# A decoder block on one Trainium2 core: the down products of its feed-forward stage with tokens on the output partitions, and its last group finished tile by tile

## The chip, the core and the metric

The kernel runs on one core of a Trainium2 chip. Its time is the device time of one execution in microseconds (us). A profile records when each instruction of the five engines ran: TensorE (PE for its matmuls, PEld for its weight loads), VectorE (DVE), ScalarE (ACT), GpSimd (POOL) and SyncE (SP, which only issues DMAs here). The span is the time from the first to the last recorded instruction. The matmul computes out = stationary.T @ moving: the stationary operand is 128x128 and is loaded into the array, the moving operand (128 x 256 or 128 x 512 in this kernel) streams through it, and the partitions of the output are the columns of the stationary operand.

## What is computed

One decoder block on x of 512 tokens x 2048 columns, in float32. The part that matters here is its end; what stands before (normalisation, one input projection, two kinds of attention, output projection) is left out.

```python
S, D_MODEL, FFN_HIDDEN = 512, 2048, 5632
...
hn2 = rmsnorm(h, norm2_g[l])
h = h + (jax.nn.silu(hn2 @ w_gate[l]) * (hn2 @ w_up[l])) @ w_down[l]
return rmsnorm(h, final_g)        # x * rsqrt(mean(x*x) + 1e-6) * g, over the 2048 columns
```

## The kernel before

**Precision.** Each float32 operand of a matmul is split into a high and a low part (float32r), and a product is three matmuls: high x high, high x low, low x high (`mm3` at L297 to L299, `mm` at L302 to L304). The high part of a weight tile is written by ACT (L176, `Job.first`), the low part by DVE (L190, `Job.second`); a Twin does the same for two half-size pieces (L210 on ACT, L214 on DVE). The products of blocks are grouped in Strassen's way: seven products of sums of blocks (P1 to P7) instead of eight.

**Order.** All work is laid out by hand. `jobs` lists the weight tiles in the order in which TensorE uses them; `next_half` hands out the next split tile and first makes ACT and DVE split a few tiles ahead. `later(n, f)` issues f when n more tiles have been handed out, `soon` and `tick` do so by the number of products. DMAs of weights are issued on SP in the order of `units`, into five buffers `raw`; DMAs that add to memory go through POOL.

**The feed-forward stage.** The hidden 5632 columns are 44 slices f of 128 (FB = 44), in groups of PH = 4. For each f the seven quad products (gate and up, 24 matmuls of 128x256 each) run, and the results become activations of 128 hidden columns x 512 tokens. When a group of four slices is done, its down products follow, mixed into the next slices: for the first ten groups, `down7` does seven products for each of 8 column blocks k, 2 x 3 matmuls each. There the weights are stationary (128 hidden x 128 output columns) and the activations move (128 hidden x 256 tokens), so the output has 128 output columns on the partitions and 256 tokens along a row. ACT copies between the banks and out to staging tiles (L1690), POOL adds these to `kept_sums` in memory (L1697).

**Places in SBUF.** Tiles start at a multiple of 256 bytes, and operands stand at a chosen offset in them, in float32 elements: activations (moving) at MH = ML = 32, which is 128 bytes, weights (stationary) at WH = WL = 16, which is 64 bytes, or with `even` at 128 bytes too:

```python
MH, ML, WH, WL = 32, 32, 16, 16
...
    def wsplit(even):
        return both(wp, 512, MH if even else WH, tag=turn("w", 5), name="w")
```

The first product P1 of the slices f = 0, 2, all odd f and all f divisible by four has its first weight tile `even`; of the down products of a group, two of the 29 Twins are `even` too (one with a single product of 6 matmuls, one with two, 12 matmuls).

**The residual and the end.** The residual h is in memory during the stage. Scaled by DVE (L1863), it is added to `kept_sums` at f = 5, 6, 9, 10, 13, 14, 17 and 18 (`add_residual`). The scale per token stands along the row there, so it is spread over the partitions by matmuls with the identity (`Spread`, L379). At f = 41 and 42 `bring_back` loads the sums into `hs`. The last group, p = 10, is done in `last` without Strassen's grouping: for each half of the tokens (256) and each of 16 column blocks, 4 x 3 matmuls of 128x256 into `pl`, a DVE addition (L1985 or L1987), a square on ACT (L1962), a sum of squares on POOL or DVE (L1964) and a multiplication by the gain on ACT (L1965). The sum over the partitions and its inverse root (`Rsqrt`, matmuls at L350) and its spreading (`Spread`, L379) go through TensorE, for the first half of the tokens amid the second half's products, for the second half after the last product; then nine scalings on DVE (L1952) with their output DMAs (L1953) end the kernel.

## Time and profile before

| | |
|---|---|
| time, median of 3 runs | 2085.97 us (2085.27 to 5372.69) |
| the profiled execution | 2088.05 us, of which the span is 2086.3 us |
| mean granted TensorE clock | 0.998 |
| busy: PE / PEld / DVE / ACT / POOL | 99% / 96% / 84% / 65% / 19% |
| matmuls | 16297 |
| feed-forward stage, from its first quad product to the last down matmul | about 797 to 2073.6 us |
| after the last down matmul | 12.7 us |

A row of a list by line has the line, engine, operation, out<-in with shapes, the count, the busy time and the mean time of one in ns, and the idle time before. A row of the table by stretch has the stretch, its length, then for each engine the busy time and (x the number of instructions), the granted clock, the share of DMA time and GB/s. A row of the timeline has the start, the duration, the engine and the instruction. Matmuls are pipelined: one lasts longer than the time between two starts, so their pace is read from the starts.

### The profile page before, as it was taken

The page shows a single profiled execution, that of the slowest core. Times are in us where ns is not written, and L with a number is a line of the kernel's source. Part 1 is how long each engine was busy: PE and PEld are TensorE (multiplying, and loading weights), DVE is VectorE, ACT ScalarE, POOL GpSimd, SP SyncE. Part 2 cuts the span into 40 slices and gives each one's busy share as a digit, 9 for nine tenths or more (in the row PEclk, how much of TensorE's full clock was granted, in tenths as well). Part 3 has the DMA queues.
Part 4 walks back from the last instruction along what each step waited for, and adds up shares of the span by engine and source line. Part 5 has one row for each costly group of instructions (what it writes and reads, how often), then busy time and mean ns, then how long its engine had stood idle before and what let it go on. Part 6 is the DMA issues. An engine that isn't in the chain of part 4 may idle for free.

```text
span 2086.3 us, 44180 instructions
## 1 busy us (share of the span) xinstructions
PE 2070.6 (99%) x16297; PEld 1993.7 (96%) x16297; DVE 1752.7 (84%) x3831; ACT 1355.5 (65%) x3355; POOL 389.3 (19%) x487
## 2 busy tenths in 40 slices
PE   9999999999999999999999999999999999999998
PEld 8789999999988889999999999999999999999997
DVE  6778888788887589989989898988889898888885
ACT  6566666566664356585767667685857676676856
POOL 0011111111120002021322213130303122030323
PEclk9999999999999999999999999999999999999999
DMA  7466665666564235366776869694847567494982
GB/s 243 156 208 163 164 154 135 168 155 146 146 217 161 97 106 175 109 215 161 185 190 168 211 146 225 152 213 118 210 130 189 147 169 175 133 211 123 217 245 94
DMA packets 138298, 351.02 MB, mean 168 GB/s; under 512 B 15328, under 2 KB 39392, under 8 KB 138080
## 3 DMA queue, kind: packets, MB, share of 16 engines
q1 hardware_dynamic: 76384, 235.44, 33.8%
q0 software_dynamic: 61552, 112.69, 29.1%
q8 instruction: 128, 2.10, 0.4%
q14 instruction: 90, 0.74, 0.1%
q10 hardware_dynamic: 144, 0.07, 0.0%
HBM read 268.89 MB, written 72.35 MB: 164 GB/s over the span
## 4 chain that ended last, share of the span: by engine, by line
PE 95%; DVE 2%; DMA 2%; ACT 1%; issue 0%; POOL 0%; SPq 0%; DVEq 0%; POOLq 0%; ACTq 0%
PE P L302 18%; PE P L304 18%; PE P L303 18%; PE pp L304 5%; PE pp L302 5%; PE pp L303 5%; PE pab L298 3%; PE pab L299 3%; PE pab L297 3%; PE pd L302 1%; PE pd L303 1%; PE pd L304 1%; PE pt L969 1%; PE pp L299 1%; PE pp L298 1%; PE pp L297 1%
## 5 line engine op out<-in xcount | busy, mean ns | idle before, releaser
L176 ACT ACTIVATE w<-raw 128x512 fp32r<-128x512 f32 (+2 forms) x1058 | 598.7, 594 | 300.5 <-DVE raw L1348 121.3
L190 DVE TENSOR_TENSOR w<-raw,w 128x512 fp32r<-128x512 f32 (+2 forms) x1024 | 659.3, 658 | 112.0 <-ACT w L176 109.7
L302 PE MATMUL P<-ah,w 128*128 128x256 f32 x1616 | 447.1, 277 | 0.0
L304 PE MATMUL P<-ah,w 128*128 128x256 f32 x1616 | 447.1, 277 | 0.0
L303 PE MATMUL P<-al,w 128*128 128x256 f32 x1616 | 446.8, 276 | 0.0
L304 PEld LDWEIGHTS P<-ah,w 128*128 128x128 f32 x1616 | 303.5, 188 | 0.3 <-DVE w L190 0.2
L302 PEld LDWEIGHTS P<-ah,w 128*128 128x128 f32 x1616 | 303.6, 188 | 0.1
L303 PEld LDWEIGHTS P<-al,w 128*128 128x128 f32 x1616 | 303.5, 188 | 0.0
L1697 POOL DMA_DIRECT2D sums<-stg x240 | 198.3, 874 | 429.1 <-ACT P L1690 150.8
L214 DVE TENSOR_TENSOR w<-raw,w 128x256 fp32r<-128x256 f32 x480 | 186.7, 420 | 28.2 <-ACT w L210 26.1
L1348 DVE TENSOR_TENSOR raw<-raw 128x512 f32<-128x512 f32 x274 | 188.5, 688 | 3.4
L210 ACT ACTIVATE w<-raw 128x256 fp32r<-128x256 f32 x480 | 177.0, 410 | 4.8 <-DVE raw L1426 4.8
L302 PE MATMUL pp<-ah,w 128*128 128x256 f32 (+1 forms) x544 | 164.1, 302 | 0.5 <-DVE pp L726 0.5
L304 PE MATMUL pp<-ah,w 128*128 128x256 f32 (+1 forms) x544 | 160.3, 295 | 1.5 <-DVE w L190 1.1
L303 PE MATMUL pp<-al,w 128*128 128x256 f32 (+1 forms) x544 | 159.2, 293 | 0.0
L1690 ACT ACTIVATE stg<-P 128x256 f32<-128x256 f32 x280 | 105.5, 381 | 15.3 <-DMA sums<-stg 5.8
L304 PEld LDWEIGHTS pp<-ah,w 128*128 128x128 f32 x544 | 102.3, 188 | 6.0 <-DVE w L190 2.9
L1352 POOL DMA_DIRECT2D raw<-in_wst_dram x40 | 34.3, 859 | 379.5 <-ACT w L176 174.9
L302 PEld LDWEIGHTS pp<-ah,w 128*128 128x128 f32 x544 | 102.7, 189 | 2.6 <-issue 0.6
L303 PEld LDWEIGHTS pp<-al,w 128*128 128x128 f32 x544 | 102.6, 189 | 1.9
L302 PE MATMUL pp<-T,w 128*128 128x256 f32 x357 | 101.7, 285 | 0.0
L297 PE MATMUL pab<-ah,w 128*128 128x512 f32 x256 | 100.6, 393 | 0.0
(399 smaller groups left out, 6161.7 us busy)
## 6 DMA issues: line engine op xcount, KB each, us to landing
raw<-in_wst_dram SPq DMA_DIRECT2D x390, 512.0 KB, 4.3
sums<-stg POOLq DMA_DIRECT2D x160, 256.0 KB, 7.0
raw<-in_wst_dram POOLq DMA_DIRECT2D x34, 448.0 KB, 6.6
raw<-in_wst_dram POOLq DMA_DIRECT2D x40, 256.0 KB, 4.7
sums<-stg POOLq DMA_DIRECT2D x80, 128.0 KB, 6.5
xc<-in_xt_dram SPq DMA_DIRECT2D x16, 256.0 KB, 3.5
bias<-in_bias_dram SPq DMA_DIRECT2D x16, 256.0 KB, 3.6
hs<-in_xt_dram SPq DMA_DIRECT2D x16, 256.0 KB, 5.2
```

The costliest lines, as they stand in the source:

```text
L176: act.activation(h, src, AF.Copy, scale=sign)
L190: dve.tensor_tensor(l, src, h.bitcast(F32), op=OP.subtract)
L210: act.activation(h, src(), AF.Copy)
L214: dve.tensor_tensor(l, src(), h.bitcast(F32), op=OP.subtract)
L297: pe.matmul(o, wh, mh, start=start, stop=False)
L298: pe.matmul(o, wh, ml, start=False, stop=False)
L302: pe.matmul(o, wh, mh, start=start, stop=False, skip_group_check=True)
L303: pe.matmul(o, wh, ml, start=False, stop=False, skip_group_check=True)
L304: pe.matmul(o, wl, mh, start=False, stop=stop, skip_group_check=True)
L1348: return lambda: dve.tensor_tensor(o(), o(), x(), op=OP.add)
L1690: return lambda: act.activation(o, a, AF.Copy)
L1697: return lambda s=sums[x]: pool_e.dma_start(kept_sums[k][:, q:q + n, :], s, **how)
```

## The change

The output of the down products is turned round. The activations become the stationary operand (128 hidden x 128 tokens), the weights the moving one, so that an output has 128 tokens on its partitions and output columns along a row. The parts are these.

- **Down products of the first ten groups**: a weight tile of one product is now 128x512 (two blocks of 128x256), used for two products with t = 0 and 1 (two times 128 tokens). The 29 Twins of a group become 28 Jobs of 128x512; there are again 336 matmuls of 128x256 in a group. No down tile is `even` any more. The activations stand at 0 modulo 256 bytes (`hx`, `x3`), the weight tiles at 64 bytes.
- **Residual**: at f = 5 to 18 it is loaded, transposed in blocks of 32x32 by DVE (`turn_residual`) and stored as rows of tokens (`kept_rows`); at f = 21 to 34 it is loaded from there, scaled by ACT with one number per partition, and added to `kept_sums` by POOL. The `Spread` of its scale at f = 0 goes. The columns stand in the order TURN in the weights, the gain and the output.
- **Slice f = 4** takes ORDER1, with which one sum of weight blocks comes from a POOL DMA.
- **The last group** goes over four token tiles t and four column blocks d of 512: 12 matmuls of 128x512 each. For t = 0 and 1 both tiles use a weight tile as it comes, and the residual is added by DVE; for t = 2 and 3 ACT writes the residual into the bank first (`seed`) and the matmuls add to it. The last block is done as two halves of 256. Squares are summed along the row by ACT itself (`accum_out`), so no matmul is in the norm; `norm` is a chain on one column per token tile. The gain is loaded as a full tile (2 x 512 KB).

```diff
+    hx = [slot[x][:, 12 * S + 64:KB * S + 64].rearrange("p (a b) -> p a b", b=S) for x in "hl"]
...
-        return ORDER0 if not f else ORDER1 if f in (1, 5, 9, 13, 17) or 4 < f <= FB - PH and f % PH in (3, 0) else ORDER
+        return ORDER0 if not f else ORDER1 if f in (1, 5, 9, 13, 17) or 3 < f <= FB - PH and f % PH in (3, 0) else ORDER
...
-    def kept(nb):
+    def kept(n):
         def f():
-            m = {6: 15, 15: 6}.get(nb, nb)
-            t, n = ("", m) if m < 8 else ("B11" if m < 12 else "T1", m % 4)
-            return tuple(slot[t + x][:, at + 512 * n:at + 512 * n + 512]
-                         for x, at in (("h", MH if nb == 6 else WH), ("l", ML if nb == 6 else WL)))
+            t, m = (("B11", 0), ("", 4), ("T1", 0), ("", 0))[n // 4]
+            c = 512 * (m + n % 4)
+            return tuple(slot[t + x][:, at + c:at + c + 512] for x, at in (("h", WH), ("l", WL)))
         return f
...
+            comb(q(1), q(1), q(2))
...
-        jobs.append(Twin([quarter(p, k, name) for k, name in items], even))
+            comb(q(3), q(3), second[m])
+
+        n, prep, post = {"P1": (0, None, sums13), "P2": (3, None, None), "P6": (2, sum2, None), "P5": (1, None, None),
+                         "P7": (0, None, lambda: load_to(u + RB + 1)), "P3": (3, sum4, None),
+                         "P4": (2, None, lambda: load_to(u + RB + 2))}[name]
+        return Job(lambda: second[m] if name == "P6" else q(n), prep=prep, post=post)
+
+    def downs(p, items):
+        for m, name in items:
+            sched.append(("s", p, (m, name)))
+            jobs.append(quarter(p, m, name))
 
...
-            seq = sorted(((k, n) for k in range(8) for n in DTIME), key=lambda x: 7 * x[0] + DTIME[x[1]])
+            seq = [(m - (n == "P4"), n) for m in range(4) for n in DOWN if m or n != "P4"] + [(3, "P4")]
             if name == "P3" and f and f % PH == 0:
-                downs(p, seq[:1], True)
+                downs(p, seq[:1])
             sched.append(("q", f, name))
             jobs += qj[2 * i:2 * i + 2]
             if name == "P3" and f and f % PH == 0:
-                for n in range(1, len(seq) - 1, 2):
-                    downs(p, seq[n:n + 2], n == 19)
+                downs(p, seq[1:-1])
...
-    RESIDUAL = {f: 2 * i for i, f in enumerate((5, 6, 9, 10, 13, 14, 17, 18))}
+    TURNED = {f: 2 * i for i, f in enumerate((5, 6, 9, 10, 13, 14, 17, 18))}
+    RESIDUAL = {f: 2 * i for i, f in enumerate((21, 22, 25, 26, 29, 30, 33, 34))}
...
-        b1, b2, b3, b4 = (b[:, :256] for b in roles[k % 2])
+        b1, b2, b3, b4 = (b[:, :256] for b in roles[t])
         o = {"P1": b1, "P2": b1, "P6": b2, "P3": b2, "P7": b3, "P4": b3, "P5": b4}[name]
-        th, tl = parts[name]
+        th, tl = (a[:, :, 128 * t:128 * t + 128] for a in parts[name])
         for i in range(2):
-            c = slice(128 * i, 128 * i + 128)
-            mm(o, wh[:, c], wl[:, c], th[:, i, :], tl[:, i, :], i == 0 and name in ("P1", "P5"), i == 1)
+            c = slice(256 * i, 256 * i + 256)
+            mm(o, th[:, i, :], tl[:, i, :], wh[:, c], wl[:, c], i == 0 and name in ("P1", "P5"), i == 1)
...
-            copy(b2, b1)()
+            if m == 0 and t:
+                later(0, copy(b2, b1))
+            else:
+                copy(b2, b1)()
...
+    def turn_residual(n):
+        q, half, part = n // 4, n // 2 % 2, n % 2
         t = st["pool"].tile([128, 2, 256], F32, tag="stga", name="res", bufs=3)
-        tv = t.rearrange("p t c -> p (t c)")
-        sp.dma_start(tv, kept_hs[nb])
+        for k in range(2):
+            sp.dma_start(t[:, k, :], kept_hs[4 * q + 2 * part + k][:, 256 * half:256 * half + 256])
+        o = rest["early"].rearrange("p (b c) -> p b c", c=128)
+
+        def turn():
+            for k in range(2):
+                c = 64 * part + 32 * k
+                dve.transpose(o[:, :, c:c + 32], t[:, k, :].rearrange("p (b i) -> p b i", i=32))
+            if part:
+                for a in range(4):
+                    c = 512 * a + 128 * q
+                    sp.dma_start(kept_rows.rearrange("(b j) d -> j b d", j=32)[:, 8 * half:8 * half + 8, c:c + 128],
+                                 o[32 * a:32 * a + 32, :, :])
+
+        later(4, turn)
+
+    def add_residual(n):
+        t = st["pool"].tile([128, 2, 256], F32, tag="stga", name="res", bufs=3)
+        a, c = rows_of(n)
+        sp.dma_start(t, kept_rows.rearrange("(b p) d -> p b d", p=128)[:, a::2, c])
 
         def scale():
-            dve.scalar_tensor_tensor(tv, tv, 1.0 if nb < 8 else -1.0, st["inv"], op0=OP.mult, op1=OP.mult)
-            pool_e.dma_start(mem_at(nb), t, accum_op=OP.add)
+            inv = st["inv"][n % 2]
+            for i in range(2):
+                act.activation(t[:, i, :], t[:, i, :], AF.Copy, scale=inv[:, a + 2 * i:a + 2 * i + 1])
+            pool_e.dma_start(mem_at(n), t, accum_op=OP.add)
 
         later(4, scale)
...
-            st["x3"] = [placed(pool, 3 * S, at, name="x3" + x) for x, at in (("h", MH), ("l", ML))]
+            st["x3"] = [placed(pool, 3 * S, 0, name="x3" + x) for x in "hl"]
...
+            st["hs"] = pool.tile([128, 4, D], F32, name="hs")
+            st["gain"] = pool.tile([128, 1024], F32, name="gain"), rest["early"]
+            st["cols"] = pool.tile([128, 4, 16], F32, name="cols")
+        if n == 15:
+            for k in range(2):
+                sp.dma_start(st["gain"][k], gain_in[:, 1024 * k:1024 * k + 1024])
...
-            for s, (k, name) in enumerate(b):
-                c = slice(256 * s, 256 * s + 256)
-                down7(a, k, name, h[:, c], l[:, c])
+            for t in range(2):
+                down7(a, b[0], t, b[1], h, l)
...
-                later(1, lambda r=r: st.update(inv=Spread(r.z), r2=Spread(r.y)))
+                minus = r.rs[:, 3, 4:8]
+                dve.tensor_scalar(minus, r.z, -1.0, None, op0=OP.mult)
+                st["inv"] = r.z, minus
+                later(1, lambda r=r: st.update(r2=Spread(r.y)))
-                inv, pinv = st["inv"], st["inv"](False, room=True)
-                inv = inv.r
-                st["inv"] = inv
-                later(5, lambda: act.activation(inv, pinv, AF.Copy))
...
+        def seed(p, t, d, a=0, n=W):
+            act.activation(p[:, :n], hs[:, t, chunk(d, a, n)], AF.Copy, scale=1.0 if d < 2 else -1.0)
+            return p
...
+        def product(p, t, d, i, a=0, n=W):
+            wh, wl = (x[:, a:a + n] for x in w[PH * d + i])
+            th, tl = (x[:, i, 128 * t:128 * t + 128] for x in hx)
+            mm(p[:, :n], th, tl, wh, wl, t < 2 and i == 0, i == PH - 1)
+
+        def square(p, t, j, n=W):
+            junk = ft("sq")
+            act.activation(junk[:, :n], p[:, :n], AF.Square, accum_out=cols[:, t, j:j + 1])
...
+        def summed(p, t, d):
+            h = hs[:, t, chunk(d)]
+            dve.tensor_tensor(h, p, h, op=OP.add if d < 2 else OP.subtract)
+            square(h, t, d)
...
+        def after_one(t, d):
+            square(banks[t, d], t, d)
+            gained(banks[t, d], t, d)
+            for _ in range(2):
                 if todo:
                     scaled(*todo.popleft())
...
+        tail = []
+        for (t, d), nxt in zip(order, ahead):
+            if type(nxt) is int:
+                tail.append(seed(new(), 3, 3, 256 * nxt, 256))
+            else:
+                banks[nxt] = seed(new(), *nxt)
+            for i in range(PH):
+                product(banks[t, d], t, d, i)
+            after_one(t, d)
+            if (t, d) == (2, 3):
+                total(2), norm(2)
+                todo.extend((2, d, act if d == 3 else dve) for d in range(PH))
+        for k, p in enumerate(tail):
+            for i in range(PH):
+                product(p, 3, 3, i, 256 * k, 256)
+            square(p, 3, 3 + k, 256)
+            if k == 0:
+                while todo:
+                    scaled(*todo.popleft())
+                total(3)
+        norm(3)
+        r = cols[:, 3, 10:11]
+        for k in (1, 0):
+            c = chunk(3, 256 * k, 256)
+            dve.scalar_tensor_tensor(hs[:, 3, c], tail[k][:, :256], r, gained_by(c), op0=OP.mult, op1=OP.mult)
+        sp.dma_start(out[3, :, chunk(3)], hs[:, 3, chunk(3)])
+        scaled(3, 0, act)
+        scaled(3, 2)
+        scaled(3, 1, act)
```

Three places of the program show what moves. The first is ACT in the middle of a group's down products. `w<-raw` rows write the high part of a weight tile, rows into `stg` copy a finished bank out, and rows between `P`, `pd` and `P` copy from bank to bank (the numbers behind P tell the banks apart). Before:

```order
L210 ACTIVATE w<-raw 128x256 x2
L1690 ACTIVATE stg<-P_9189 128x256
L1690 ACTIVATE stg<-P_9188 128x256
L210 ACTIVATE w<-raw 128x256
L210 ACTIVATE w<-s_15601 128x256
L1690 ACTIVATE pd<-P_9186 128x256
L1690 ACTIVATE stg<-P_9185 128x256
L210 ACTIVATE w<-raw 128x256 x2
L1690 ACTIVATE stg<-pd 128x256
L1690 ACTIVATE P_9189<-P_9184 128x256
L210 ACTIVATE w<-raw 128x256 x2
```

and after the change:

```order
L178 ACTIVATE w<-raw 128x512
L1700 ACTIVATE stg<-pd 128x256
L1700 ACTIVATE stg<-P_9185 128x256
L178 ACTIVATE w<-raw 128x512
L1700 ACTIVATE stg<-P_9186 128x256
L1700 ACTIVATE stg<-P_9189 128x256
L178 ACTIVATE w<-s_15644 128x512
L1700 ACTIVATE P_9186<-P_9188 128x256
L1700 ACTIVATE P_9189<-P_9184 128x256
L178 ACTIVATE w<-raw 128x512
L1700 ACTIVATE stg<-pd 128x256
L1700 ACTIVATE stg<-P_9185 128x256
```

Two splits of 128x256 for two products have become one split of 128x512; two copies of 128x256 still stand between one split pair and the next.

The second is TensorE at the end of the program, the last matmuls of the last group (`pl`). Before:

```order
L297 MATMUL pl<-ah 128x256
L298 MATMUL pl<-al,ah 128x256
L299 MATMUL pl<-ah,al 128x256
L350 MATMUL prs<-ones,sacc 128x32 x2
L350 MATMUL prs<-ones,sqt 128x32 x2
L379 MATMUL prb<-ident,rs 128x128 x2
```

and after:

```order
L304 MATMUL pl<-T1h,ah 128x512
L305 MATMUL pl<-T1l,ah 128x512
L306 MATMUL pl<-T1h,al 128x512
L304 MATMUL pl<-ah 128x256
L305 MATMUL pl<-al,ah 128x256
L306 MATMUL pl<-ah,al 128x256
```

The matmuls of 128x512 end where the two halves of the last block begin (24 matmuls of 128x256), and the norm's matmuls (`prs`, `prb`) are gone: nothing of TensorE's follows the last product.

The third is DVE at the end of the program, from the last products on. Before:

```order
L1987 TENSOR_TENSOR hs<-pl,hs 128x256
L358 SCALAR_TENSOR_TENSOR rs<-prs,rs 128x2
L360 RECIPROCAL rs<-rs 128x2
L361 SCALAR_TENSOR_TENSOR rs<-rs 128x2
L362 TENSOR_TENSOR rs<-rs 128x2
L363 SCALAR_TENSOR_TENSOR rs<-rs 128x2
L1952 TENSOR_TENSOR scaled<-hs,prb 128x256 x2
L1952 TENSOR_TENSOR scaled<-hs,prb 128x512 x7
```

and after:

```order
L2017 TENSOR_TENSOR hs<-pl,early 128x512
L2021 TENSOR_TENSOR cols<-cols 128x2
L2022 TENSOR_TENSOR cols<-cols 128x1
L2023 SCALAR_TENSOR_TENSOR cols<-cols,rs 128x1
L2031 SCALAR_TENSOR_TENSOR cols<-cols 128x1
L2033 RECIPROCAL cols<-cols 128x1
L2034 SCALAR_TENSOR_TENSOR cols<-cols 128x1
L2035 TENSOR_TENSOR cols<-cols 128x1
L2036 SCALAR_TENSOR_TENSOR cols<-cols 128x1
L2122 SCALAR_TENSOR_TENSOR hs<-pl,cols,early 128x256 x2
L2052 TENSOR_SCALAR hs<-hs,cols 128x512
```

The chain on columns (`cols`, one element per partition) is followed by two multiplications of 128x256 from the last two banks and one of 128x512, in place of nine; ACT does two more of 128x512 beside it.

248 lines of the change are left out of this document (136 added, 112 removed).

## The prediction

> **What bounds the kernel now.** The page comes first, its busy times and its chain of waits.
>
> ```profile
> PE 2070.6 (99%) x16297; PEld 1993.7 (96%) x16297; DVE 1752.7 (84%) x3831; ACT 1355.5 (65%) x3355; POOL 389.3 (19%) x487
> ...
> PE 95%; DVE 2%; DMA 2%; ACT 1%; issue 0%; POOL 0%; SPq 0%; DVEq 0%; POOLq 0%; ACTq 0%
> ```
>
> TensorE carries 95% of the chain that ended last, so the question is how fast it starts matmuls, and what runs after the last one. The table by stretch shows, in order: slices with quad products alone, the same piece later, one group's down products, slice f = 4, the last group, and the end.
>
> ```profile
> core 0: us, PE busy (x) PEld busy (x) DVE busy (x) ACT busy (x) POOL busy (x), PEclk, DMA share, GB/s
> 1512.00:1582.88 70.88, 70.88 (x626) 70.88 (x625) 62.72 (x115) 40.88 (x85) 4.29 (x5) 1.00 0.49 134
> 1741.20:1814.21 73.01, 73.01 (x627) 72.91 (x625) 63.67 (x116) 41.41 (x85) 4.27 (x5) 1.00 0.48 131
> 1586.32:1623.12 36.80, 36.80 (x326) 36.80 (x325) 32.31 (x80) 33.53 (x106) 18.05 (x22) 1.00 0.97 222
> 883.00:894.80 11.80, 11.80 (x101) 11.60 (x99) 11.15 (x22) 8.09 (x18) 0.00 (x0) 1.00 0.28 93
> 2027.01:2073.56 46.55, 46.52 (x398) 46.12 (x396) 30.61 (x68) 36.01 (x80) 19.50 (x24) 1.00 0.24 81
> 2073.56:2086.27 12.71, 2.46 (x12) 1.97 (x12) 6.20 (x16) 1.29 (x4) 0.00 (x0) 0.61 0.44 166
> ```
>
> The first two rows hold the same 26 products of 24 matmuls (624). They differ by 2.13 us at the same granted clock, 1.00, with PE busy throughout. The timeline says why; read the distances of the starts (first column).
>
> ```profile
> 1600.46 0.28 PE L303 MATMUL P<-al,w 128*128 128x256 f32 x1
> 1605.90 0.28 PE L303 MATMUL P<-x3l,w 128*128 128x256 f32 x1
> 1743.47 2.07 DVE L190 TENSOR_TENSOR w<-raw,w 128x512 fp32r<-128x512 f32 x3
> 1744.04 0.28 PE L303 MATMUL P<-al,w 128*128 128x256 f32 x1
> 1744.21 0.39 PE L304 MATMUL P<-ah,w 128*128 128x256 f32 x1
> 1744.44 0.28 PE L302 MATMUL P<-ah,w 128*128 128x256 f32 x1
> 1749.74 0.28 PE L302 MATMUL P<-ah,w 128*128 128x256 f32 x1
> 1755.39 0.28 PE L302 MATMUL P<-ah,w 128*128 128x256 f32 x1
> 1797.82 0.28 PE L302 MATMUL P<-B11h,w 128*128 128x256 f32 x1
> 2007.89 0.28 PE L302 MATMUL P<-B11h,w 128*128 128x256 f32 x1
> 2009.33 0.28 PE L302 MATMUL P<-B11h,w 128*128 128x256 f32 x1
> 700.10 0.39 PE L297 MATMUL pab<-ah,w 128*128 128x512 f32 x1
> 709.62 0.39 PE L297 MATMUL pab<-ah,w 128*128 128x512 f32 x1
> ```
>
> There are four paces. **Quick**: 48 matmuls of 128x256 in 5.44 us, 113.3 ns each. **Slow**: from 1749.74, 48 in 5.65 us, 117.7 ns. **Even** (the tile w of P1 at 128 bytes, like the activations): 12 in 1.44 us, 120.0 ns. **Wide**: 42 of 128x512 in 9.52 us, 226.7 ns, twice the quick one. The slow stretch begins behind a stall: the first of three low parts (DVE, from 1743.47, about 0.69 us each) ends at 1744.16, the matmul that needs it starts at 1744.21, and from then the pace is slow, until an even tile comes at 1797.82; behind it the quick pace is back. So a short wait costs its own 0.2 us (1744.04 to 1744.44 for two matmuls) and then 4.4 ns per matmul. Nearly all of the stage runs quick: the room is small.
>
> **The change part by part**, against the profiled execution (2088.05 us, span 2086.3; 2.1 us above the median shown).
>
> *1. Matmul count.* A group has 336 matmuls of 128x256 before and after: nothing. The last group has 384 of 128x256 before, 180 of 128x512 and 24 of 128x256 after. By the paces 384 x 113.3 = 43.5 us, and 180 x 226.7 + 24 x 113.3 = 43.5 us. Width alone gives nothing. Here the Trainium skill speaks otherwise: TensorE: Matmul & The Clock Gate, section Back-to-back issue gap, gives an isolated matmul N/2.4 + 2.5 ns, so that wide ones save the fixed 2.5 ns; by it this term would be about -0.5 us (an estimate). The trace, with 226.7 = 2 x 113.3, shows no fixed part.
>
> *2. The last group's waits.* It takes 46.55 us now, with a slow stretch and the norm of the first half (Rsqrt and Spread) inside. After the change no matmul stands in the norm, the fourth weight tile is needed 3 x 6 x 226.7 ns = 4.1 us into the group, not 1.0, and each token tile and block gives DVE and ACT 12 x 226.7 ns = 2.72 us, for three DVE instructions of about 0.69 us and ACT's square and seed at some 0.6 us each (rows below). I take 43.5: **-2.9 us** (bounds 0, and -3.0).
>
> *3. Even tiles of down products.* 6 + 12 matmuls in each of 10 groups at 120.0 instead of 113.3 ns: **-1.2 us**, if the others stay quick.
>
> *4. Weight splitting.* The rows that price it:
>
> ```profile
> L190 DVE TENSOR_TENSOR w<-raw,w 128x512 fp32r<-128x512 f32 x421 | 285.8, 688 | 66.2 <-ACT w L176 64.8
> L176 ACT ACTIVATE w<-raw 128x512 fp32r<-128x512 f32 x420 | 252.6, 626 | 113.5 <-DVE raw L1348 83.8 <-DMA raw<-in_wst_dram 12.8 <-PE P L304 11.1
> L214 DVE TENSOR_TENSOR w<-raw,w 128x256 fp32r<-128x256 f32 x336 | 130.7, 420 | 19.6 <-ACT w L210 18.1
> L210 ACT ACTIVATE w<-raw 128x256 fp32r<-128x256 f32 x336 | 123.9, 410 | 3.6 <-DVE raw L1426 3.6
> L1419 DVE TENSOR_TENSOR raw<-raw 128x512 f32<-128x512 f32 x56 | 38.8, 692 | 1.9
> L1863 DVE SCALAR_TENSOR_TENSOR res<-res,r 128x512 f32<-128x512 f32 x13 | 8.9, 685 | 0.0
> ```
>
> For a pair of column blocks DVE has 14 x 420 + 2 x 692 + 4 x 420 (the half-size sums) = 8.9 us, after 7 x 688 + 4 x 692 = 7.6 us; ACT 14 x 410 = 5.7, after 7 x 626 = 4.4. Four pairs free 5.5 us of DVE and of ACT in the 36.80 us of a group, in which both were busy for 32.31 and 33.53. TensorE did not wait there, so this is worth only the stalls that a late DVE causes behind a group: the 2.13 us stretch, and the one at f = 4, where 96 matmuls take 11.80 us in place of 10.9 (its count takes in those at the edges) and where ORDER1 takes a sum off DVE. I take both: **-3.0 us** (bounds 0 and -3.0).
>
> *5. New alignment.* Activations stationary at 0, weights moving at 64 bytes. The trace has moving minus stationary 64 bytes (128 and 64, quick or slow) and 0 bytes (128 and 128, even); the pair (64, 0) is not in it. Bounds: 113.3 and 120.0 ns, so 0 to +22 us for 3360 matmuls and 0 to +2.4 for the wide ones. I take 113.3, since the distance is that of the quick row. At the 60 changes between quad and down products one matmul each meets a new distance: 60 x 6.7 ns = **+0.4 us**. The first group begins behind a seed matmul, with no even tile until the next P1: 336 x 4.4 ns = **+1.5 us**.
>
> *6. Residual.* The first Spread at f = 0 is gone, half of this row: **-0.9 us**.
>
> ```profile
> 815.00 1.79 PE prb L379 x16
> ```
>
> A transposition of 128x256 on DVE isn't in the trace; the nearest row of its size has 420 ns. Two of them replace one L1863 row: 16 x (840 - 685) ns = 2.5 us, hidden in DVE's 8.2 idle us per 70.88 of quad slices (four per stretch: 0.6 us). At 1.37 us each the cover would be gone. ACT's scaling, 32 x 410 ns, lies in slices where ACT is busy for 40.88 of 70.88 us. Its loads and stores, and 1 MB of gain ahead of the last weights on SP's queue, meet a DMA share of 0.49 in those slices: nothing.
>
> *7. The end.* The rows from the last matmul on, and the price of a read of ACT's row sum:
>
> ```profile
> 2073.59 0.42 DVE L1987 TENSOR_TENSOR hs<-pl,hs 128x256 f32<-128x256 f32 x1
> 2075.18 0.16 DVE L358 SCALAR_TENSOR_TENSOR rs<-prs,rs 128x2 f32<-128x2 f32 x1 [1.17 <-PE prs L350]
> 2076.20 0.16 DVE L363 SCALAR_TENSOR_TENSOR rs<-rs 128x2 f32<-128x2 f32 x1
> 2077.74 4.94 DVE L1952 TENSOR_TENSOR scaled<-hs,prb 128x256 f32<-128x256 f32 x9 [1.38 <-PE prb L379]
> 2078.19 4.85 SPq L1953 DMA_DIRECT2D out_dram<-scaled  x9
> 2079.00:2085.00 6.00, 0.00 (x0) 0.00 (x0) 3.68 (x7) 0.00 (x0) 0.00 (x0) 0.50 0.92 350
> L905 ACT ACTIVATION_READ_ACCUMULATOR e<-e,st 128x1 f32 x96 | 18.3, 190 | 0.0
> ```
>
> Now: from 2073.56 the end takes 12.7 us. After: square 0.42 and read 0.19, the chain on one column 1.2 (2075.18 to 2076.36), two multiplications of 128x256 at 0.42, one of 128x512 at 0.69: the last DVE instruction ends 3.4 us after the last matmul, and the first of four output DMAs starts at 2.6. Four of 256 KB at 350 GB/s take 3.0 us, with 1 us before the first data and 1.3 after the last (as now: issue at 2078.19, first data in the stretch from 2079, end of the data about 2085.0, of the span 2086.27). 2.6 + 1 + 3.0 + 1.3 = 7.9, rounded down to 7.5 as DMAs overlap DVE: **-5.2 us** (bounds -6 and 0).
>
> Sum: -2.9 - 1.2 - 3.0 + 0.4 + 1.5 - 0.9 - 5.2 = **-11.3 us**, span 2075.0, profiled execution 2076.8; from the median shown, 2085.97 - 11.3 = **2074.7 us**.
>
> **The rivals.**
>
> *A. The quick pace is lost at the changes of operand places (slower than before).* For: every stall in the rows above led to the slow pace, and a quad matmul at 128 bytes now runs while a tile at 0 is loaded, a distance (128) that the stage did not have. Against: the step from distance 64 to 0 and back at even tiles keeps the quick pace. Price: if slow, a group has 12 + 24 + 312 matmuls until the next even tile and 324 behind it until the one after: 672 x 4.4 ns = 3.0 us, ten times, and 1.7 us in the last group: +31.3, of which 1.5 is counted. 2074.7 + 29.8 = 2104.5 us. It decides from 38% of those matmuls on (11.3 / 29.8).
>
> *B. The pair (64, 0) is itself as slow as even tiles.* Then 22.4 + 2.4 = +24.8: 2099.5 us. For: no row shows it. Against: same distance as the quick rows.
>
> *C. DVE late through transpositions.* At over 1.37 us each, eight slices stall, each as at 1744 with a slow stretch (about 1 us for half a stretch, the 2.13 us above): +8, so 2083.
>
> *D. The end doesn't shrink*, because four DMAs of 256 KB in a row land one by one at 2.5 us: 2080. Against: 0.92 DMA share with 350 GB/s in the row above.
>
> ```profile
> out_dram<-scaled SPq DMA_DIRECT2D x7, 256.0 KB, 2.5
> L304 PEld LDWEIGHTS P<-ah,w 128*128 128x128 f32 x1126 | 211.5, 188 | 0.1
> ```
>
> *E. Wide matmuls run faster*, down to the 188 ns of a weight load in the second row: 180 x (226.7 - 188) = -7.0, 2067.7. Against it: the wide row's 226.7 ns. The same section of TensorE: Matmul & The Clock Gate gives a sustained 131 ns for N=512, by which it would be -17 us (an estimate); the trace's 226.7 disagrees.
>
> **How the numbers follow.** Forecast 55% (2066 to 2080), A 20% (2080 to 2105, by the share that is lost), B 8%, C 7%, D 5%, E 3%, others 2%. The predicted time is that of the first, 2075 us. The range 2066 to 2097 leaves out the upper half of A, B and the others, and the low edge. About 2% is what a measurement of this kernel can tell: faster than 2044.3 or slower than 2127.7 is reached by no case listed, so 2% each for what I don't see.
>
> **What would show it.** Right: down products (L304 to L306 in the new numbering) at 113.3 ns from start to start, the last group near 43.5 us, the end under 8 us, no wait of PE behind groups. Wrong: 117.7 or 120 ns in the down products (A, B), waits for low parts of w in slices f = 5 to 18 (C), or an end of over 10 us (D).

## The result, and the profile after

| | before | after |
|---|---|---|
| time, median | 2085.87 us | 2108.53 us (2106.87 to 2109.21) |
| ratio, 95% interval | | 1.0108 [1.0089, 1.0128] |
| the profiled execution / its span | 2088.05 / 2086.3 us | 2109.19 / 2107.1 us |
| mean granted clock | 0.998 | 0.999 |

The change makes the kernel 1.1% slower; the forecast was 0.5% faster, and the time lies outside the range. (Of the runs of before, the one of 5372.69 us is an outlier that the ratio leaves out.) The prediction put at about 2% what a measurement of this kernel can tell; the interval here reaches 0.2% to either side, so the loss is clear. The page of after, busy times and chain of waits:

```profile
PE 2091.1 (99%) x16085; PEld 2006.5 (95%) x16085; DVE 1723.8 (82%) x3481; ACT 1335.6 (63%) x3089; POOL 373.0 (18%) x465
...
PE 91%; DVE 3%; DMA 3%; issue 2%; ACT 1%; POOL 0%; SPq 0%; ACTq 0%; POOLq 0%; DVEq 0%
```

DVE, ACT and POOL have less to do, TensorE has 212 matmuls fewer and is busy for 20.5 us longer. So its matmuls start further apart. The tables by stretch say where: first the slices ahead of the ten groups and the ten groups of before, then these two, the last group and the end of after.

```profile
797.34:894.55 97.21, 97.21 (x841) 97.04 (x840) 90.58 (x175) 58.59 (x120) 9.50 (x17) 1.00 0.43 147
894.55:2027.01 1132.46, 1132.46 (x9941) 1132.20 (x9939) 1001.29 (x2043) 784.84 (x1999) 262.10 (x308) 1.00 0.72 179
```

```profile
797.91:893.78 95.87, 95.24 (x834) 95.04 (x832) 89.15 (x174) 57.66 (x118) 11.23 (x19) 1.00 0.49 154
893.78:2054.68 1160.90, 1159.69 (x9940) 1158.80 (x9939) 978.08 (x1700) 775.79 (x1751) 263.86 (x308) 1.00 0.74 183
2054.68:2098.89 44.21, 44.19 (x206) 36.59 (x204) 30.22 (x70) 24.69 (x61) 0.00 (x0) 1.00 0.32 108
2098.89:2107.10 8.21, 0.00 (x0) 0.00 (x0) 2.07 (x8) 2.12 (x5) 0.00 (x0) 0.77 0.39 128
```

Against before: +0.6 us ahead of all this, -1.3 in the slices, **+28.4 in the ten groups** (the expectations below say 28.6, from a start 0.2 us later in before), -2.3 in the last group (46.55), -4.5 at the end (12.71). That makes the +20.8 us between the spans, to 0.1. In the groups there are as many matmuls as before (the counts differ by one at the edges), and the clock is 1.00 in both. One group of after, stretch by stretch (counts take in matmuls at the edges), in the order in which they come: the main run of 312 down matmuls, the even tile, the next tile of quad products (12), and, behind 12 more down matmuls, 312 quad matmuls and then 156.

```profile
1134.65:1171.40 36.75, 36.75 (x315) 36.75 (x313) 28.75 (x45) 30.47 (x78) 17.29 (x20) 1.00 0.98 216
1171.40:1172.83 1.43, 1.43 (x15) 1.43 (x13) 0.85 (x2) 1.43 (x5) 0.63 (x2) 1.00 1.11 231
1172.83:1174.19 1.36, 1.36 (x14) 1.36 (x13) 1.36 (x3) 0.33 (x1) 1.09 (x2) 1.00 1.12 205
1175.60:1212.35 36.75, 36.75 (x315) 36.75 (x313) 31.72 (x61) 20.60 (x43) 1.72 (x2) 1.00 0.63 185
1213.78:1231.46 17.68, 17.68 (x158) 17.68 (x157) 16.14 (x31) 11.07 (x22) 1.74 (x2) 1.00 0.63 161
```

Divide by the counts: 117.8 ns, 119 (even), **113.3**, 117.8, and 113.3 again behind the even tile at 1212.35. The quick tile between is the telling one. The timeline of TensorE shows its edges:

```profile
1172.83 0.28 PE L304 MATMUL P<-B11h,w 128*128 128x256 f32 x1
1174.19 0.28 PE L304 MATMUL pd<-w,x3h 128*128 128x256 f32 x1
1175.60 0.28 PE L304 MATMUL P<-T4h,w 128*128 128x256 f32 x1
```

Twelve quad matmuls take 1.36 us, the next twelve, down products, 1.41, with no wait between. Without a stall the pace goes from quick to slow where the operands change places, and it stays slow when they change back. That is the pattern of rival A, and in the trace every one of the ten groups has such a quick tile with slow matmuls behind it.

### The profile page after: what moved, and what is told of

Same layout as the page of the kernel before. It is cut to its first block, busy times and chain, and to the rows that moved or that the text cites. A ratio compares the mean times of both kernels' runs of the same rounds, so it can differ in the third digit from the quotient of the medians.

```text
span 2107.1 us, 43221 instructions
## 1 busy us (share of the span) xinstructions
PE 2091.1 (99%) x16085; PEld 2006.5 (95%) x16085; DVE 1723.8 (82%) x3481; ACT 1335.6 (63%) x3089; POOL 373.0 (18%) x465
## 4 chain that ended last, share of the span: by engine, by line
PE 91%; DVE 3%; DMA 3%; issue 2%; ACT 1%; POOL 0%; SPq 0%; ACTq 0%; POOLq 0%; DVEq 0%
PE P L304 17%; PE P L306 17%; PE P L305 17%; PE pp L306 5%; PE pp L304 5%; PE pp L305 5%; PE pab L300 3%; PE pab L301 3%; PE pab L299 3%; DMA raw<-in_wst_dram 1%; PE pd L305 1%; PE pd L306 1%; PE pd L304 1%; PE pt L971 1%; DVE w L192 1%
## 5 line engine op out<-in xcount | busy, mean ns | idle before, releaser
L192 DVE TENSOR_TENSOR w<-raw,w 128x512 fp32r<-128x512 f32 (+1 forms) x1264 | 823.6, 663 | 183.8 <-ACT w L178 180.0
L178 ACT ACTIVATE w<-raw 128x512 fp32r<-128x512 f32 (+2 forms) x1298 | 749.1, 600 | 302.0 <-DVE raw L1350 119.9
L306 PE MATMUL P<-ah,w 128*128 128x256 f32 x1056 | 293.7, 278 | 0.3 <-DVE w L192 0.3
L304 PE MATMUL P<-ah,w 128*128 128x256 f32 x1056 | 293.8, 278 | 0.0
L305 PE MATMUL P<-al,w 128*128 128x256 f32 x1056 | 293.3, 278 | 0.0
L306 PEld LDWEIGHTS P<-ah,w 128*128 128x128 f32 x1056 | 198.4, 188 | 0.9 <-DVE w L192 0.7
L304 PEld LDWEIGHTS P<-ah,w 128*128 128x128 f32 x1056 | 198.2, 188 | 0.0
L305 PEld LDWEIGHTS P<-al,w 128*128 128x128 f32 x1056 | 197.9, 187 | 0.0
L304 PE MATMUL P<-w,ah 128*128 128x256 f32 x560 | 156.6, 280 | 0.9 <-ACT P L1700 0.9
L305 PE MATMUL P<-w,ah 128*128 128x256 f32 x560 | 156.7, 280 | 0.0
L306 PE MATMUL P<-w,al 128*128 128x256 f32 x560 | 156.4, 279 | 0.0
L304 PEld LDWEIGHTS P<-w,ah 128*128 128x128 f32 x560 | 105.1, 188 | 1.1 <-ACT P L1700 1.1
L305 PEld LDWEIGHTS P<-w,ah 128*128 128x128 f32 x560 | 105.2, 188 | 0.0
```

Source lines behind the costliest of these rows:

```text
L178: act.activation(h, src, AF.Copy, scale=sign)
L192: dve.tensor_tensor(l, src, h.bitcast(F32), op=OP.subtract)
L304: pe.matmul(o, wh, mh, start=start, stop=False, skip_group_check=True)
L305: pe.matmul(o, wh, ml, start=False, stop=False, skip_group_check=True)
L306: pe.matmul(o, wl, mh, start=False, stop=stop, skip_group_check=True)
```

## The experiments

Two theories were left. **A**: the quick pace is lost where the operand places change. **B**: the new pair, moving at 64 and stationary at 0 bytes, is slow by itself. In the trace of after each stretch of that pair also stands behind a change, so it can't tell them apart. Each median below stands with its ratio to the kernel before, run on the same chip; where no ratio stands, there is one run, and only the paces in its trace are read. A place is written (moving, stationary) in bytes modulo 256.

**1. The kernel before, moved as a whole to the new pair.**

```diff
-MH, ML, WH, WL = 32, 32, 16, 16
+MH, ML, WH, WL = 16, 16, 0, 0
```

> The kernel before, with all operand places moved down by 64 bytes: moving at 64 and stationary at 0 where it was 128 and 64, even tiles at 64 where they were at 128. Order, tiles and stalls are the same. Theory A (only a change of places, or a stall, loses the quick pace): the same time as before, 2086 us within 5 us, median gap between the 256-column matmuls 113.3 ns. Theory B (the pair 64 and 0 is slow by itself): 10465 matmuls x 4.4 ns = +46 us, about 2132 us.

2089.93 us, 1.0022 [1.0012, 1.0031]. The ten groups:

```profile
897.10:2028.76 1131.66, 1131.66 (x9940) 1131.48 (x9939) 1001.74 (x2043) 785.30 (x1999) 262.43 (x308) 1.00 0.71 179
```

1131.66 us at the pair (64, 0), where (128, 64) took 1132.46. B falls: the pair is as quick as the old one. (An even tile of this kernel has both operands at 64.) In its profile the groups begin 2.5 us later than before; what this move costs lies ahead of them.

**2. The changed kernel with one pair throughout.** The other products' operands go to (64, 0) too.

```diff
-MH, ML, WH, WL = 32, 32, 16, 16
+MH, ML, WH, WL = 16, 16, 0, 0
...
-        return Job(lambda: second[m] if name == "P6" else q(n), prep=prep, post=post)
+        return Job(lambda: second[m] if name == "P6" else q(n), prep=prep, post=post, even=True)
```

(With `even` a down tile is at 16 elements, 64 bytes, as in after; `kept` likewise.)

> The changed kernel with one pair of places throughout: the operands of the other products are moved down by 64 bytes, so that they too have the moving operand at 64 and the stationary one at 0 bytes, like the down products; tiles, order and instructions are the same. Theory A (a change of places loses the quick pace): the ten groups have nothing left that loses it but real stalls, so some 25 us of the 28.6 us that the groups gained go, about 2083 us. Theory B (the pair 64 and 0 is slow by itself): now the other products are slow as well. In the changed kernel 6928 of them average 115.7 ns; at 117.7 they cost 6928 x 2.0 ns = +14 us, about 2122 us, and more in the stages ahead.

2087.95 us, 1.0008 [0.9997, 1.0020]. The ten groups, and a run of 480 matmuls of both kinds, quad and down, without an even tile in it:

```profile
896.53:2030.60 1134.07, 1132.87 (x9941) 1132.02 (x9939) 976.72 (x1700) 772.83 (x1751) 263.96 (x308) 1.00 0.75 187
1110.96:1165.36 54.40, 54.40 (x483) 54.40 (x481) 46.50 (x78) 42.28 (x102) 19.00 (x22) 1.00 0.81 187
```

1134.07 in place of 1160.90 us, and 480 matmuls in 54.40 us, 113.3 ns. With tiles, order and instructions the same, 26.8 of the 28.4 us go with the places alone, as read from the profiled executions. The exchange of roles is still in this kernel (the weights move, the activations are stationary), so it is not the cause. By the medians the whole kernel gets back 20.6 of its 22.7 us: its runs spread from 2081.61 to 2092.50 us, the profiled one (2085.01) is among the quicker, and the stages ahead take 2.8 us longer in it.

**3. The kernel before, with one tile a group at another place.** The Twin that was even goes to 0 bytes.

```diff
-        return both(wp, 512, MH if even else WH, tag=turn("w", 5), name="w")
+        return both(wp, 512, 0 if even == 2 else MH if even else WH, tag=turn("w", 5), name="w")
...
-                    downs(p, seq[n:n + 2], n == 19)
+                    downs(p, seq[n:n + 2], 2 if n == 19 else False)
```

> The kernel before, with the one down tile of each group that stood at distance 0 (both operands at 128 bytes) placed at 0 bytes instead, so 128 bytes from its moving operand; nothing else differs. Theory A in its wide form (any tile at another distance than the one before it, other than 0, loses the quick pace until a tile at distance 0): from that tile to the even tile of the next group some 204 matmuls are slow, 204 x 4.4 ns x 10 = +9 us, 2095 us. Theory B (a pair has its own pace, and a change by itself does nothing): the tile runs at the pace of its own pair, 24 matmuls x 10 at 113 to 120 ns, and the rest as before: 2084 to 2088 us.

2108.22 us, 1.0107 [1.0092, 1.0122]: 12 matmuls a group at another place cost as much as the whole change. Ahead of the tile (132 matmuls), behind it (204), the even tile, behind that (330), and behind the next even tile (156):

```profile
1130.06:1145.02 14.96, 14.96 (x134) 14.96 (x133) 14.68 (x39) 13.21 (x44) 4.70 (x6) 1.00 0.72 190
1146.44:1170.47 24.03, 24.03 (x207) 24.03 (x205) 19.24 (x46) 21.34 (x66) 12.07 (x16) 1.00 1.09 241
1170.47:1171.91 1.44, 1.44 (x14) 1.44 (x13) 0.43 (x2) 1.24 (x3) 1.33 (x2) 1.00 1.18 201
1171.91:1210.77 38.86, 38.86 (x332) 38.86 (x331) 33.91 (x62) 21.54 (x45) 4.78 (x5) 1.00 0.72 188
1212.20:1229.88 17.68, 17.68 (x158) 17.68 (x157) 16.49 (x32) 11.10 (x22) 2.92 (x3) 1.00 0.65 147
```

113.3, 117.8, even, 117.8, even, 113.3 ns. A, but 2.5 times the +9 us expected: here an even tile did not restore the pace, only the second one did. So it is in nine of the ten groups. In one, with a stall ahead of the tile (at 1603 us), the first even tile did restore it; in another with a stall ahead (at 1024 us) it did not. (9 x (204 + 330) + some 300) x 4.4 ns = 22.5 us, and 22.6 were lost.

**4. Tiles at distance 0 behind the changes.** In the changed kernel the first tile of each main down run goes to 0 bytes, where the stationary operand is, and the quad products behind the short down runs get an even tile.

```diff
+        r["P3", 0].even = f % PH == 0 and f > 0
+        r["P4", 0].even = f % PH == 1 and f > PH
...
-        return Job(lambda: second[m] if name == "P6" else q(n), prep=prep, post=post)
+        head = first.pop((p, m, name), False)
+        return Job(lambda: second[m] if name == "P6" else q(n), prep=prep, post=post,
+                   dst=(lambda: both(wp, 512, 0, tag=turn("w", 5), name="w")) if head else None)
...
+        if len(items) > 1:
+            first[(p,) + items[0]] = True
```

> The changed kernel, with the first weight tile of each main run of down products placed at 0 bytes, where the stationary activations are (distance 0, the pace of 120.0 ns), and with one weight tile of the products behind that run placed at 128 bytes, where their activations are; nothing else differs. The places still change twice a group. Theory A (the quick pace of 113.3 ns is lost where the operand places change, and comes back behind a tile at distance 0): the down products run at 113.3 from their second tile on, 3264 x 4.4 ns = -14.4 us, the products behind them run at 113.3 from their own such tile on, 312 x 4.4 ns x 10 = -13.7 us, and some 40 even tiles cost 40 x 12 x 6.7 ns = +3.2 us: 2108.5 - 25 = 2083.6 us. Theory B (moving operand at 64 and stationary at 0 bytes is a slow pair by itself, 117.7 ns wherever it stands): only the second part is won, 2108.5 - 13.7 + 3.2 = 2098 us, and the down products stay at 117.7 ns behind their first tile.

2094.76 us, 1.0043 [1.0028, 1.0058], between the two expectations: 300 down matmuls behind the tile at 0 bytes, and 300 quad matmuls behind an even tile:

```profile
1132.04:1167.60 35.56, 35.56 (x302) 35.40 (x301) 27.27 (x43) 28.40 (x73) 17.29 (x20) 1.00 1.00 209
1173.23:1207.23 34.00, 34.00 (x303) 34.00 (x301) 31.30 (x61) 19.52 (x40) 0.84 (x1) 1.00 0.68 196
```

The quad products are quick again (113.3 ns), the down products are not (117.8, without the 0.2 us of a short wait). A tile with the moving operand moved onto the stationary one, (0, 0), doesn't do what (128, 128) does. By itself this looks like B; the first two experiments exclude B.

**5. Other heads, group by group.** The same edit with a table of places for the first one to four down tiles.

> The changed kernel with another treatment of the first tiles of the main down run in each of its ten groups, read group by group from the pace of the some 300 matmuls behind them (without it they take 117.7 ns, and behind one tile at 0 bytes as well). Bytes of the moving weight tile, the stationary operand at 0: group 0 one tile at 192, group 1 one at 128, group 2 two at 192, group 3 two at 0, group 4 two at 0 with a usual tile between, group 5 four at 0, group 6 one at 32, group 7 one at 96, group 8 one at 224, group 9 one at 160. Theory A1 (a tile brings the quick pace back only if its moving operand lies where it stays, so that only the stationary one moves): slow in all ten groups. Theory A2 (every tile at distance 0 moves the pace one step on, and a second one brings it back): 113.3 ns in groups 3, 4 and perhaps 5, slow in the rest. In time each group that comes back to 113.3 ns is worth 300 x 4.4 = 1.3 us, so 2095 to 2109 us in all.

2109.15 us, one run. All ten stay slow; behind four tiles at 0 (group 5), for instance, 264 matmuls take

```profile
1492.34:1523.44 31.10, 31.10 (x267) 31.10 (x265) 23.39 (x37) 25.99 (x68) 16.16 (x19) 1.00 1.09 226
```

117.8 ns. A2 falls (two or four tiles at distance 0 bring nothing back). A1 is not contradicted here.

**6. A map, in the kernel before.** The tile of experiment 3 goes to another place in each group.

```diff
-                    downs(p, seq[n:n + 2], n == 19)
+                    downs(p, seq[n:n + 2], TILES[p].get(n, False))
```

> The kernel before, with the down tile that stood at distance 0 in the middle of each group at another place in each group, read group by group from the 204 matmuls behind it and the 330 behind the next tile at distance 0. Bytes of the stationary weight tile, the moving operand at 128: group 0 at 0, group 1 at 192, group 2 at 32, group 3 at 96, group 4 two tiles at 0, group 5 one at 0 and the next at 128, group 6 one at 0 and the next two at 128, group 7 at 160, group 8 at 224, group 9 none moved (all at 64). Theory A in its wide form (any other distance than 64 or 0 loses the pace): slow in groups 0 to 8, quick in 9. Theory A1 (a tile with only the stationary operand moved onto the moving one restores it): groups 5 and 6 quick behind their tile at 128. Theory A2 (a tile at distance 0 moves the pace one step, and two are needed behind a tile at 0): group 5 slow for its run and quick behind the next even tile, group 6 quick at once. Each group that stays slow for 534 matmuls costs 534 x 4.4 = 2.3 us: 2090 to 2108 us.

2092.86 us, one run. Behind the tile at 192, 32 and 96 bytes, at 0 and then 128 bytes (192 matmuls), and at 160 and 224 bytes:

```profile
1029.45:1052.57 23.12, 23.12 (x206) 23.12 (x205) 19.19 (x47) 21.38 (x66) 12.10 (x15) 1.00 1.12 255
1144.60:1167.72 23.12, 23.12 (x207) 23.12 (x205) 19.14 (x46) 21.30 (x66) 11.93 (x16) 1.00 1.10 248
1259.16:1282.28 23.12, 23.12 (x207) 23.12 (x205) 19.14 (x47) 21.34 (x66) 12.03 (x15) 1.00 1.10 244
1492.14:1513.90 21.76, 21.76 (x195) 21.76 (x193) 17.70 (x43) 19.95 (x62) 11.58 (x15) 1.00 1.10 245
1720.61:1744.64 24.03, 24.03 (x207) 24.03 (x206) 19.24 (x46) 21.20 (x66) 12.22 (x15) 1.00 1.10 240
1836.08:1860.11 24.03, 24.03 (x207) 24.03 (x206) 19.24 (x46) 21.34 (x66) 12.21 (x15) 1.00 1.10 241
```

113.3 ns for the first four, 117.8 for the last two (and the next even tile restores these): A in its wide form falls. In group 9 the tile stands at 64 bytes like the others, so that no tile of the main run is even, and the pace stays quick for its 324 matmuls and the 24 quad matmuls ahead of them:

```profile
1935.06:1974.50 39.44, 39.44 (x350) 39.44 (x349) 34.92 (x88) 35.85 (x113) 18.02 (x22) 1.00 0.96 224
```

A stationary tile at 32, 96 or 192 bytes keeps the pace behind it, one at 0, 160 or 224 loses it, and a tile at 128 directly behind one at 0 restores it at once (A1 says so, A2 not). But behind 0 bytes (group 0, and two such tiles in group 4) and 204 slow matmuls the even tile failed, as in experiment 3, and A1 doesn't explain that. Group 6, one tile at 0 and two at 128, comes back to 113.3 ns too, but a stall stands ahead of it.

**7. Other places for the down operands.** The pair of the down products stays 64 bytes apart but stands elsewhere; HX is where `hx` and `x3` begin, DW the weight tiles, both in elements: 48 and 0, 56 and 8, 32 and 48.

```diff
-    hx = [slot[x][:, 12 * S + 64:KB * S + 64].rearrange("p (a b) -> p a b", b=S) for x in "hl"]
+    hx = [slot[x][:, 12 * S + HX:KB * S + HX].rearrange("p (a b) -> p a b", b=S) for x in "hl"]
...
+                   dst=lambda: both(wp, 512, DW, tag=turn("w", 5), name="w"))
```

> The changed kernel with the stationary activations of the down products at 192 bytes and their moving weights at 0, instead of 0 and 64: again 64 bytes apart, again both places change twice a group; tiles, order and instructions are the same. Theory C (what counts is the pair at the seam: the last moving operand at the old place beside the first stationary one at the new place; moving minus stationary at 128, 160 and 224 bytes lost the pace in the map, 0, 32, 96 and 192 kept it): going in, 128 - 192 = 192 modulo 256, coming out, 0 - 64 = 192, both keep it, so the ten groups are quick and the kernel takes 2108.5 - 25 = 2083.5 us. Rival A (every change of both places loses it): 2108 us as the changed kernel.

> The same with the stationary activations at 224 and the moving weights at 32 bytes, 64 apart too. Theory C: going in, 128 - 224 = 160, coming out, 32 - 64 = 224, both lose the pace: 2108 us, down products and those behind them at 117.7 ns. If the kernel with 192 and 0 bytes was quick for another reason (places above the old ones, or a gap between the operands of 64 downward), this one is quick as well, 2083 us.

> The same with the stationary activations at 128 and the moving weights at 192 bytes. Theory C: going in, 128 - 128 = 0, keeps the pace, coming out, 192 - 64 = 128, loses it: the down products run at 113.3 ns and the products behind them at 117.7 ns up to the next tile at distance 0, half of the loss, 2108.5 - 3264 x 4.4 ns = 2094 us. Rival A: 2108 us, both at 117.7 ns.

2107.36, 2108.75 and 2107.13 us (1.0107 [1.0090, 1.0124], 1.0112 [1.0092, 1.0132], 1.0104 [1.0084, 1.0124]). Theory C falls with the first: at (0, 192) the 12 down matmuls that come out of a quick stretch are slow at once.

```profile
1128.37:1129.79 1.42, 1.42 (x15) 1.42 (x13) 1.28 (x3) 0.62 (x2) 0.00 (x0) 1.00 0.00 0
```

The third has one quick piece. At (192, 128): 12 down matmuls out of a quick stretch, the 24 quad matmuls behind them, the main down run:

```profile
1130.06:1131.43 1.37, 1.37 (x15) 1.37 (x13) 1.28 (x3) 0.57 (x2) 0.00 (x0) 1.00 0.01 3
1131.43:1134.25 2.82, 2.82 (x26) 2.82 (x25) 2.70 (x6) 2.22 (x7) 0.00 (x0) 1.00 0.72 216
1134.25:1171.00 36.75, 36.75 (x315) 36.75 (x313) 28.71 (x45) 29.91 (x76) 17.29 (x20) 1.00 0.99 217
```

114, 117.5 and 117.8 ns: moving both operands up by 64 bytes keeps the pace, moving them back loses it, and the main run comes out of a slow stretch. This can be put to use.

**8. Up by 64 bytes, and an even tile on the way back.** The third kernel of experiment 7 with the two even quad tiles of experiment 4.

> The changed kernel with the stationary activations of the down products at 128 and their moving weights at 192 bytes, and two more weight tiles a group at distance 0 (both operands at 128 bytes), right behind the two places where the order comes back from a short down run; the long run has such a tile behind it already. The runs with other places showed that a move of both operands up by 64 bytes keeps the quick pace and the move back loses it until a tile at distance 0. If that is the rule, every stretch is quick: 2107.1 - 25 + 20 x 12 x 6.7 ns (1.6 us) = 2084 us, with the places still changing. Theory A in its wide form (each change of both places loses it): the down runs stay at 117.7 ns and only the products behind them come back, 2107.1 - 12.2 = 2095 us, as in the kernel with tiles at distance 0 at the heads of the runs.

2084.39 us, 0.9994 [0.9985, 1.0003]. The main down run (312) and the quad products behind the next short one (300):

```profile
898.07:933.43 35.36, 35.36 (x315) 35.36 (x313) 28.43 (x46) 30.94 (x79) 10.82 (x20) 1.00 0.69 239
939.02:973.02 34.00, 34.00 (x302) 34.00 (x301) 30.19 (x59) 19.31 (x40) 0.01 (x1) 1.00 0.54 174
893.48:2030.77 1137.29, 1135.23 (x9940) 1133.81 (x9939) 976.85 (x1700) 772.01 (x1751) 263.87 (x308) 1.00 0.75 187
```

113.3 ns in both, with 60 changes of places as in after. So a change of places need not cost the pace: it depends on which change it is, and on an even tile behind the one that loses it. The last row, the ten groups, is still 4.8 us above before; the section on the reasons takes it up.

**9. One pair, from the feed-forward stage on.** Experiment 2 with the stages ahead left at (128, 64): quad and down jobs are placed 16 elements lower, and so are the activations of the quad products.

> The changed kernel with one pair of places (moving at 64, stationary at 0) from the first feed-forward product on, and the stages ahead left as they were; order, tiles and instructions are the same. The kernel with the places moved throughout had the ten groups at the quick pace and lost some 2.8 us in the stages ahead. Theory A (the loss is all from the changes of places): the last step from the changed kernel to here is -20.6 -2.8 us, 2085 us, the same as the kernel before within 3 us, with the gains of the end (4.5 us) and of the last group (2.6 us) eaten by the stalls at the changes of stage in the groups. Its rival (the gain of the shifted kernel came from the stages ahead): 2105 us or more.

2085.28 us, 0.9993 [0.9982, 1.0005]: as A has it, and the rival named there falls. (The runs spread from 2079.92 to 2092.86 us.)

**10. The version that the runs point to.** Experiment 9 with the even tiles of experiment 4 on the quad products and, at the end,

```diff
-            (sp if e is not act else act).dma_start(out[t, :, c], h)
+            sp.dma_start(out[t, :, c], h)
```

> The version that the runs point to: one pair of places (moving at 64, stationary at 0) from the first feed-forward product on, one more weight tile at distance 0 ahead of each main down run and one behind it, and the last two output transfers issued by SP instead of ACT. In the kernel without the added tiles two stalls, at 1565 and 1684 us, left 816 and 480 matmuls at 117.7 ns, (816 + 480) x 4.4 ns = 5.7 us. If a tile at distance 0 restores the pace there as it did elsewhere, most of that goes, and the 20 tiles cost 20 x 12 x 6.7 ns = 1.6 us: 2085.3 - 3 = 2082 us, 3 us under the kernel before. If such a tile restores it only every second time, as it did at 1623 us, nothing is left: 2085 us.

2082.74 us, 0.9986 [0.9976, 0.9997]: the lowest of these medians, 0.1% under the kernel before. Stalls of up to 1.2 us came again in its profile; behind two of them some 200 matmuls were slow, behind the others the pace stayed quick. The expectation's price for the stalls was misread: in the trace of experiment 9 the two stand at 1583.2 and 1701.2 us, with some 670 and 330 slow matmuls behind them, so 4.4 us and not 5.7. The edits were not tried apart.

## Why the prediction was wrong, step by step

**Step 5, the alignment, is the one that failed: +1.9 us were counted, and the ten groups lost 28.4.** Its first half was right: the pair (64, 0) does take 113.3 ns (experiments 1 and 2), the price of the nearest row. Its second half was not: "one matmul each meets a new distance" took the pace for a property of the pair under way. The prediction's own rows showed otherwise, since a stall of 0.2 us had cost 4.4 ns on each of hundreds of later matmuls: the pace depends on what came before, and a change of places is such an event. The 28.4 us add up: 672 matmuls a group x 4.4 ns x 10 = +29.6, less 2.1 for some 470 matmuls that were slow in before too, less 1.2 for the even down tiles (step 3), and +2.0 of stalls (step 4), 28.3 in all. Rival A had that mechanism, the count of 672 and nearly the time (2104.5), and got 20%. What spoke against it there, the harmless step from distance 64 to 0 and back at even tiles, bears on a move of the stationary operand alone onto the moving one, and no further.

That A's count came out is in part luck, for it takes each even tile to restore the pace. That is so in the ten groups of after, but not in general, and the rows of before that the prediction read had an exception: it let the slow stretch from 1744 us end at "an even tile" at 1797.82, but there is one at 1778.01 already, behind which 156 matmuls still take 117.8 ns each.

```profile
1778.01:1779.45 1.44, 1.44 (x15) 1.44 (x13) 1.44 (x3) 0.63 (x1) 0.00 (x0) 1.00 0.05 11
1779.45:1797.82 18.37, 18.37 (x159) 18.37 (x157) 16.36 (x31) 11.02 (x22) 1.72 (x2) 1.00 0.52 128
```

**Steps 1 and 2, width and last group: -2.9 predicted, -2.3 measured.** The 180 wide matmuls start 41.20 us after the first (2054.68 to 2095.88 in the timeline), 228.9 ns each and not 226.7: +0.4 us. They took the same in experiment 2, where the pace ahead was quick, so rival A's extra 1.7 us for this group was not there. Rival E fell: no two of them start less than 225 ns apart, where the Trainium skill (TensorE: Matmul & The Clock Gate, section Back-to-back issue gap) gives 131 ns for this width.

**Step 3, the even tiles,** can't be seen by itself: 18 matmuls a group no longer pay 6.7 ns each. What the term left out is that an even tile can end a slow stretch: in before the one at 1026 us does so behind a stall. Where no pace was lost it is not needed, as group 9 of experiment 6 shows.

**Step 4, fewer stalls: -3.0 predicted.** One part came: the stall at f = 4 is gone, and the 132 matmuls between the last even tile and the groups take 14.96 us in place of 15.61 (this is part of the -1.3 of the slices). In the ten groups the sign was wrong. The work of DVE and ACT there fell (1001.29 to 978.08 us, 784.84 to 775.79), but beside the seed matmul at the start, which both kernels have, there are five stalls, 2.4 us beyond the pace, where before had two, 0.4 us. ACT's waits for the staging buffers, in the ten groups of before and of after (us in all, times, longest):

```profile
ACT stg L1690 <- DMA sums<-stg: 7.1, 10, 1.3
```

```profile
ACT stg L1700 <- DMA sums<-stg: 17.9, 22, 1.9
```

ACT waited 22 times instead of 10 for POOL's additions to memory to land, and while it waits, the copy of the next bank is late. The worst one, in after, ends in a stall of TensorE:

```profile
1034.59 0.38 ACT L1700 ACTIVATE stg<-P 128x256 f32<-128x256 f32 x1 [1.94 <-DMA sums<-stg]
1036.43 0.66 ACT L1700 ACTIVATE P<-P 128x256 f32<-128x256 f32 x2
1036.88 0.39 PE L304 MATMUL P<-w,ah 128*128 128x256 f32 x1 [0.88 <-ACT P L1700]
```

In the kernel of experiment 8, where the changes of places no longer cost the pace, the stalls remain: 1137.29 against 1132.46 us. Of the 4.8 us some 0.4 are even tiles (+1.6 -1.2). Eight stalls, of 0.2 to 1.2 us beyond the pace, make 4.0 in place of the 0.4 of before, and some 600 matmuls behind them are slow, in place of 470 (+0.6). How many of the stalls go back to the staging buffers was not tried.

**Step 6, the residual: -0.9 predicted, nothing got.** The `Spread` at f = 0 is gone, but TensorE then stands waiting for a bank one step later:

```profile
819.91 0.39 PE L304 MATMUL P<-B11h,w 128*128 128x256 f32 x1 [0.63 <-DVE ft L1846]
```

The slices ahead of the groups are 1.3 us shorter all the same, since stretches of before at the slow pace there are quick now: the one behind the stall at f = 4 (0.65 us, step 4), and 156 matmuls behind the even tile at 819.45 us, which failed to restore the pace in before (0.7 us). The transposition takes 421 ns (420 assumed); ACT's scaling takes 494 (410 assumed). Neither came with a wait, and rival C fell:

```profile
L1902 ACT ACTIVATE res<-res,rs 128x256 f32<-128x256 f32 x32 | 14.3, 494 | 0.0
L1885 DVE STREAM_TRANSPOSE early<-res 128x256 f32<-128x256 f32 x32 | 12.2, 421 | 0.0
```

**Step 7, the end: -5.2 predicted, -4.5 measured** (8.21 us); rival D fell. The sum had 7.9 us and was rounded down to 7.5 "as DMAs overlap DVE"; against 7.9 it is 0.3 short. In after, the first of the last four output DMAs is issued at 2101.43, 2.5 us after the last matmul (2.6 in the working), the last at 2102.57, and the data are through by about 2105.4; the last rows are after's stretch with data, its rest, and the end of experiment 10.

```profile
2098.97 0.38 ACT L2009 ACTIVATE sq<-pl 128x256 f32<-128x256 f32 x1 [1.00 <-PE pl L306]
2101.43 0.34 ACTq L2053 DMA_DIRECT2D out_dram<-hs  x1
2102.57 0.34 ACTq L2053 DMA_DIRECT2D out_dram<-hs  x1
2102.50:2105.00 2.50, 0.00 (x0) 0.00 (x0) 0.00 (x0) 0.04 (x1) 0.00 (x0) 0.66 1.07 343
2105.50:2107.10 1.60, 0.00 (x0) 0.00 (x0) 0.00 (x0) 0.00 (x0) 0.00 (x0) 0.50 0.01 4
2072.06:2080.44 8.38, 0.00 (x0) 0.00 (x0) 2.07 (x8) 2.01 (x5) 0.00 (x0) 0.66 0.38 125
```

The data move at 343 GB/s without a gap (DMA share 1.07), as the working had it. What is longer is the rest behind them, some 1.7 us where the working took 1.3. That ACT issues two of the DMAs itself, each in 0.34 us, looks like a delay but isn't one: in experiment 10 SP issues all four, and the end takes 8.38 us.

So of -11.3 us predicted, -2.3, -4.5 and -1.3 were there (from the last group, the end and the slices), and 28.4 us against them, of which 26.8 go with the places alone. The remaining +0.6 lies ahead of the stage.
